# Inverting the triangular blocks of an RWKV-7 layer by 16x16 on VectorE, and applying the blocks beside them on TensorE

## The chip, the cores and the metric

The kernel runs on one core of a Trainium2 chip. The metric is the device time of one execution in microseconds (us). The engines are TensorE (PE; its weight loads are PEld), VectorE (DVE), ScalarE (ACT), GpSimd (POOL) and SyncE (SP), which issues the transfers.

## What is computed

One layer of a hybrid decoder: norms, dilated attention and RWKV-7 time mixing side by side, a gated merge, and a squared-ReLU MLP, for 1024 tokens of width 1024. The RWKV-7 part has 16 heads of 64 and a state that runs over all tokens. The change touches the RWKV-7 part alone:

```python
def wkv7_scan(r, w, k, v, a, b):
    """S_t = S_{t-1} diag(w_t) + (S_{t-1} a_t) b_t^T + v_t k_t^T ; y_t = S_t r_t."""
    ...
    def step(state, inp):
        r_t, w_t, k_t, v_t, a_t, b_t = inp
        sa = jnp.einsum('bhvk,bhk->bhv', state, a_t)
        state = (state * w_t[:, :, None, :] + sa[..., None] * b_t[:, :, None, :]
                 + v_t[..., None] * k_t[:, :, None, :])
        return state, jnp.einsum('bhvk,bhk->bhv', state, r_t)
    _, ys = lax.scan(step, s0, xs)
```

## The kernel before

The scan is not run step by step. The sequence is cut into 16 chunks of 64 tokens. Inside a chunk, what each token reads of the others is a strictly triangular 64x64 system, for each chunk and head; its solution gives the chunk as one matrix, and only a product for each chunk is then left to be done in order. The 16 heads are worked in 8 pairs (`m` = 0 to 7), two heads on the 128 partitions.

A pair goes through steps that `ORDER` names by letters: P projects r, k and v (dense products, L307); E and F make the decays and features; g (`pair_gram`, L749 to L757) makes the triangular systems `lm`; V the values (L722, L729); I (`pair_inverse`) inverts; L (`pair_local`) solves; C (`pair_chain`, L874, L877) runs over the chunks in order; N normalizes; G is a gate product of another part of the layer, dense products again. Tile, the layer in which the kernel is written, plans the order of all instructions on each engine when the program is built, with priorities that follow the order in which they are written, and each engine then runs its own list in that order. Dense products of P and G that are ready stand between the small products of the other steps. Nine gates (G7 to G15) stand behind the last pair in `ORDER`.

The triangular system of a chunk has two diagonal blocks of 32x32 (index `f`) and one block of 32x32 below. `pair_inverse` first turns `lm` by VectorE's transposes (L769) so that a partition holds one block of one chunk and head: 64 partitions, 32 x 32 elements in `lb`. Then a loop over `s` from 1 to 30 eliminates column by column: a product into a scratch (L775) and an addition (L777), each (31 - s) x s elements long. GpSimd writes the diagonal (L778), and two transposes (L781) bring the inverse back as `tt`. Meanwhile TensorE transposes `bk` (L785).

`pair_local` lays four chunks each as blocks of 32 on the diagonal of 128x128 operands `bd` (`place`, L805): `bd` 0 and 2 are the inverses of the two diagonal blocks, `bd` 1 the block below. It brings the right sides into `xx` by TensorE's transposes (L816, L820) and ScalarE's copies (L817, L822). Then come three rounds for each of two heads, each of four 128x128 products in float32 (L838; two records in the trace for each product): the inverse of the first block, the block below added to the second half (L840), the inverse of the second block. Results are copied to `x[0]` (L843) and to `eh` (L845). L853 to L858 make the chunk matrices from them.

Buffers that matter: pool `f4` hands out the tiles named `lt` in rotation over `NLT` = 3 buffers; in the order of the program these are `lb`, `tt`, the two `xx`, `y` and `sq` for each pair. Tiles named `ft` rotate over `NFT` = 6. `psS` has two PSUM buffers, which the small products share, `psD` has two for the dense ones. Weights are split into two parts: ScalarE casts (L64), GpSimd or VectorE subtracts (L65); `shifted` empties a projection by ScalarE (L542) and VectorE (L543).

Of the kernel before, what the change touches and what calls it, by code (L numbers as in the profile page):

```python
# [8 lines left out]
F32 = mybir.dt.float32  # L9
# [4 lines left out]
OP = mybir.AluOpType  # L14
# [19 lines left out]
NBD, NFT, NLT, NW, NGT, NRK = 5, 6, 3, 4, 2, 4  # L34
# [15 lines left out]
class Block:  # L50
# [22 lines left out]
    def pool(self, es, name, bufs, **kw):  # L73
        if kw.get("space") is not DRAM:
            kw["reuse_waits"] = "tile"
        return es.enter_context(self.tc.tile_pool(name=name, bufs=bufs, **kw))
# [469 lines left out]
    def rwkv(self, cst, wp, psD, oS, gS):  # L546
        nc, tc = self.nc, self.tc
        with ExitStack() as es:
            pool = lambda n, b, **kw: self.pool(es, n, b, **kw)
            rc, f4, b8, psC = pool("rc", 1), pool("f4", 4), pool("b8", 3), pool("psC", 1, space=PSUM)  # L550
            psS = pool("psS", 2, space=PSUM)
            self.omu = omu = rc.tile([128, 26], F32, name="omu")
            nc.vector.tensor_scalar(omu, self.c("shift_mu", 0, 26), -1.0, 1.0, op0=OP.mult, op1=OP.add)

            half = rc.tile([128, 4, 8], F32, name="half")
            for i, nm in enumerate(("decay_w0", "iclr_a0", "k_a")):
                nc.vector.tensor_scalar(half[:, i, :], self.c(nm, 0, 8), 0.5, None, op0=OP.mult)
            nc.vector.tensor_scalar(half[:, 3, :], half[:, 2, :], -1.0, 1.0, op0=OP.mult, op1=OP.add)
            smask = rc.tile([128, 8, 64], BF16, name="smask")
            nc.gpsimd.memset(smask, 1.0)  # L560
            nc.gpsimd.memset(smask[:, :, 0:1], 0.0)
            lnb = rc.tile([128, 1], F32, name="lnb")
            nc.vector.memset(lnb, 10.0 * math.log(2.0))

            dws = rc.tile([128, S], F32R, name="dws")
            das = rc.tile([128, S], F32R, name="das")
            dgs = rc.tile([128, S], F32, name="dgs")
            t = f4.tile([128, S], F32, name="rkv", bufs=NRK)
            p = self.project(wp, psD, C_LORA)
            self.shifted(p, t, 24)  # L570
            nc.scalar.activation(t[0:64], t[0:64], AF.Tanh)
            nc.scalar.copy(dws[0:64], t[0:64])
            nc.vector.tensor_tensor(dws[64:128], t[0:64], dws[0:64].bitcast(F32), OP.subtract)
            nc.scalar.copy(das[64:128], t[64:128])
            nc.vector.tensor_tensor(das[0:64], t[64:128], das[64:128].bitcast(F32), OP.subtract)
            p = self.project(wp, psD, C_LORA + 128)
            self.shifted(p, dgs, 25)
            nc.scalar.activation(dgs, dgs, AF.Tanh, scale=0.5)
            nc.vector.tensor_scalar(dgs, dgs, 0.5, 0.5, op0=OP.mult, op1=OP.add)

            bd = [rc.tile([128, 4, 128], F32, name=f"bd{i}") for i in range(NBD)]
            for b_ in bd:
                nc.gpsimd.memset(b_, 0.0)
            st = dict(rc=rc, f4=f4, b8=b8, bd=bd, dws=dws, das=das, dgs=dgs, smask=smask, half=half, lnb=lnb,
                      wp=wp, psD=psD, psS=psS, psC=psC, oS=oS, nbd=0)
            prs, step = {}, dict(
                P=lambda m: prs.__setitem__(m, self.pair_project(st, m)),
                E=lambda m: self.pair_lora(st, prs[m], m),
                F=lambda m: self.pair_features(st, prs[m], m),
                g=lambda m: self.pair_gram(st, prs[m], m),  # L590
                V=lambda m: self.pair_values(st, prs[m], m),
                I=lambda m: self.pair_inverse(st, prs[m], m),
                L=lambda m: self.pair_local(st, prs[m], m),
                C=lambda m: self.pair_chain(st, prs[m], m),
                N=lambda m: self.pair_norm(st, prs.pop(m), m),
                G=lambda j: self.gate(wp, psD, gS, j))
            for word in ORDER.split():
                if word[0] != "G" or int(word[1:]) >= NGA:
                    step[word[0]](int(word[1:]))
# [160 lines left out]
    def pair_inverse(self, st, pr, m):  # L760

        nc = self.nc
        f4, psS = st["f4"], st["psS"]
        bk, lm, fe = pr["bk"], pr["lm"], pr["fe"]

        lb = f4.tile([64, 32, 32], F32, name="lt", bufs=NLT)
        for f in range(2):
            fs = slice(32 * f, 32 * f + 32)
            nc.vector.transpose(lb[fs], lm[fs, f].rearrange("j u t -> j t u"))  # L769
        tt = f4.tile([64, 32, 32], F32, name="lt", bufs=NLT)  # L770
        pd = tt.rearrange("u t c -> u (t c)")
        for s in range(1, 31):
            n = 31 - s
            q = pd[:, 0:n * s].rearrange("u (t c) -> u t c", c=s)
            nc.vector.tensor_tensor(q, lb[:, s + 1:32, s:s + 1].to_broadcast([64, n, s]),  # L775
                                    lb[:, s:s + 1, 0:s].to_broadcast([64, n, s]), OP.mult)
            nc.vector.tensor_tensor(lb[:, s + 1:32, 0:s], lb[:, s + 1:32, 0:s], q, OP.add)  # L777
        nc.gpsimd.memset(lb.rearrange("u t c -> u (t c)")[:, 0:1024:33], 1.0)  # L778
        for f in range(2):
            fs = slice(32 * f, 32 * f + 32)  # L780
            nc.vector.transpose(tt[fs].rearrange("s u t -> s t u"), lb[fs].rearrange("u t s -> u t s"))  # L781
        for b in range(4):
            p = psS.tile([128, 4, 128], F32, name="s")
            for c in range(4):
                nc.tensor.transpose(p[:, c, :], bk[:, 4 * b + c].rearrange("p a t -> p (a t)"), self.ident)  # L785
            for h in range(2):
                nc.scalar.copy(fe[b // 2][:, h, 4 * (b % 2):4 * (b % 2) + 4, 64:128], p[:, :, 64 * h:64 * h + 64])
        pr["tt"] = tt

    def pair_local(self, st, pr, m):  # L790

        nc = self.nc
        f4, b8, psS = st["f4"], st["b8"], st["psS"]
        ident, ar, ar4, lm, fe, tt = self.ident, pr["ar"], pr["ar4"], pr["lm"], pr["fe"], pr["tt"]
        bds, ehs = [], []
        for h in range(2):
            bd = [st["bd"][(st["nbd"] + i) % NBD] for i in range(3)]
            st["nbd"] += 3
            bds.append(bd)

        def place(i, h):
            src = (tt[0:32], lm[0:32, 1], tt[32:64])[i]
            for q in range(4):
                qs = slice(32 * q, 32 * q + 32)
                (nc.scalar.copy if q % 2 or i == 1 else nc.vector.tensor_copy)(  # L805
                    bds[h][i][qs, :, qs], src[:, 16 * h + q:16 * h + 16:4, :])

        for h in range(2):
            place(1, h)
        xx = [f4.tile([128, 2, 4, 128], F32, name="lt", bufs=NLT) for h in range(2)]  # L810
        for f in range(2):
            for h in range(2):
                p = psS.tile([128, 4, 128], F32, name="s")
                for g in range(4):
                    u = slice(16 * h + 4 * g, 16 * h + 4 * g + 4)
                    nc.tensor.transpose(p[:, g, :], lm[:, f, u, :].rearrange("p u t -> p (u t)"), ident)  # L816
                nc.scalar.copy(xx[h][:, f, :, 0:64], p[:, :, 64:128])  # L817
            p = psS.tile([128, 4, 128], F32, name="s")
# [4 lines left out]
        for h in range(2):  # L823
            place(0, h)
        xs = [[x[:, 0], x[:, 1]] for x in xx]
        for h in range(2):
# [1 line left out]
            nc.gpsimd.memset(eh[64:128, :, 64:128], 0.0)  # L828
            nc.gpsimd.tensor_copy(eh[64:128, :, 0:64], ident[64:128, None, 64:128].to_broadcast([64, 16, 64]))
            ehs.append(eh)  # L830
        for i in range(3):
            for h in range(2):
                if i == 1:
                    place(2, h)
                x = xs[h]
                p = psS.tile([128, 4, 128], F32, name="s")
                for g in range(4):
                    nc.tensor.matmul(p[:, g, :], bds[h][i][:, g, :], x[i // 2][:, g, :], start=True, stop=True)  # L838
                if i == 1:
                    nc.vector.tensor_tensor(x[1], x[1], p, OP.add)  # L840
                else:
                    if i == 0:
                        nc.scalar.copy(x[0], p)  # L843
                    for q in range(4):
                        (nc.scalar.copy if i == 2 else nc.vector.tensor_copy)(  # L845
                            ehs[h][16 * i:16 * i + 32, q:16:4, :], p[32 * q:32 * q + 32])
        for b in range(4):
            for h in range(2):
                hp = slice(64 * h, 64 * h + 64)
                p = psS.tile([128, 4, 128], F32, name="s")  # L850
# [561 lines left out]
```

## Time and profile before

| | us |
|---|---|
| median of 3 runs | 2252.92 (2249.39 to 2259.89) |
| the profiled execution | 2252.45 |
| its span, first to last instruction | 2250.7 |
| TensorE busy in the span | 2083.3 (93%) |
| VectorE | 1559.3 (69%) |
| ScalarE | 1035.0 (46%) |
| GpSimd | 602.6 (27%) |

Busy times are of the profiled execution. An engine's busy share is a mean over stages that differ: the RWKV part lies between about 480 and 1340 us, and its stretches have to be read by themselves. The granted clock tells at which share of its full speed TensorE ran. Matmul records overlap, since a product begins before the one ahead of it has ended; distances from start to start tell the pace. Shares in lists of waits are idle time of an engine just before an instruction, put down to what released it last.

### The profile page before, as it was taken

To read this page: it belongs to the slowest core of one execution; us is meant where nothing else is said; L and a number is where in the kernel's file an instruction comes from. 1 tells how busy PE (TensorE), PEld (TensorE's weight loads), DVE (VectorE), ACT (ScalarE), POOL (GpSimd) and SP (SyncE) were. 2 spreads that over 40 slices of the span, in tenths; PEclk is the share of its full clock that TensorE was granted. 3 is DMA by queue.
4 is the path that set the end of the run, shared out by engine and by line. 5 is a ranking of instruction groups with operands and counts; after the bars stand their busy time and mean duration, and the time that the engine had idled before them with its cause. 6 is when DMAs were issued, how large, how long until landed. Compare 5 with 4: busy or idle time off the path is not lost. (4 is left out here: it accounts for less than half of the span.)

```text
span 2250.7 us, 28246 instructions
## 1 busy us (share of the span) xinstructions
PE 2083.3 (93%) x10002; PEld 1621.9 (72%) x10002; DVE 1559.3 (69%) x2857; ACT 1035.0 (46%) x2018; POOL 602.6 (27%) x455
## 2 busy tenths in 40 slices
PE   6899999988999989898989999999889999999997
PEld 2676766666777767676767778877667777788886
DVE  5845555458989787878777743436876553799988
ACT  4634533445454636454554442225744443533342
POOL 2504310321313131222122122201100000788850
PEclk9999999999999999999998999999999999999999
DMA  7513311110111110101011154432544333433232
GB/s 248 181 34 99 99 40 29 59 31 22 30 33 35 31 37 27 35 29 37 24 37 34 52 179 159 128 120 84 166 156 163 113 107 111 166 130 128 88 109 75
DMA packets 156315, 194.88 MB, mean 87 GB/s; under 512 B 10729, under 2 KB 110211, under 8 KB 154127
## 3 DMA queue, kind: packets, MB, share of 16 engines
q1 hardware_dynamic: 156175, 193.08, 25.8%
q8 instruction: 79, 1.29, 0.2%
q14 instruction: 61, 0.50, 0.1%
HBM read 152.14 MB, written 40.90 MB: 86 GB/s over the span
## 5 line engine op out<-in xcount | busy, mean ns | idle before, releaser
L307 PE MATMUL d<-hh,w_h 128*128 128x512 f32 x960 | 328.2, 414 | 8.0 <-ACT w_h L64 4.6
L307 PE MATMUL d<-hl,w_h 128*128 128x512 f32 x960 | 329.5, 413 | 2.9 <-DVE hl L280 2.9
L307 PE MATMUL d<-hh,w_l 128*128 128x512 f32 x960 | 324.2, 410 | 1.4 <-DVE w_l L65 1.3
L65 POOL TENSOR_TENSOR w_l<-w_t,w_h 128x256 fp32r<-128x256 f32 x160 | 128.3, 803 | 634.0 <-ACT w_h L64 288.7
L1108 PE MATMUL m<-op 128*128 128x512 f32 x1272 | 292.0, 391 | 6.3 <-DVE big L1344 2.4
L1108 PE MATMUL m<-big,op 128*128 128x512 f32 x1152 | 276.6, 401 | 8.0 <-ACT op L64 4.1
L1108 PEld LDWEIGHTS m<-op 128*128 128x128 f32 x1272 | 239.5, 189 | 58.5 <-POOL op L65 3.4
L1108 PEld LDWEIGHTS m<-big,op 128*128 128x128 f32 x1152 | 213.9, 189 | 70.8 <-DVE u L1219 5.3
L64 ACT CAST w_h<-w_t 128x256 fp32r<-128x256 f32 x272 | 108.4, 404 | 310.3 <-PE d L307 222.7
L307 PEld LDWEIGHTS d<-hh,w_h 128*128 128x128 f32 x960 | 180.4, 192 | 47.8 <-ACT w_h L64 5.8
L307 PEld LDWEIGHTS d<-hl,w_h 128*128 128x128 f32 x960 | 181.0, 192 | 44.9 <-issue 9.4
L307 PEld LDWEIGHTS d<-hh,w_l 128*128 128x128 f32 x960 | 180.1, 191 | 42.5 <-issue 7.9
L64 ACT CAST op<-t 128x512 fp32r<-128x512 f32 (+1 forms) x152 | 113.5, 775 | 174.5 <-PE m L1108 119.3
L153 POOL TENSOR_TENSOR macc<-macc,ada_t 128x512 f32<-128x512 f32 x56 | 87.2, 1559 | 179.5 <-ACT macc L151 160.7
L65 DVE TENSOR_TENSOR op<-t,op 128x512 fp32r<-128x512 f32 (+1 forms) x125 | 117.7, 962 | 20.5 <-ACT op L64 20.3
L1281 DVE TENSOR_TENSOR big<-big,m 128x1024 f32<-128x1024 f32 x88 | 104.7, 1210 | 11.9 <-PE m L1108 11.8
L1299 POOL TENSOR_TENSOR t<-big 128x1024 f32<-128x1024 f32 x7 | 23.1, 3303 | 325.8 <-DMA big<-in_w_ff_dram 325.4
L775 DVE TENSOR_TENSOR lt<-lt 64x30 f32<-64x30 f32 (+14 forms) x240 | 97.1, 404 | 8.2
L777 DVE TENSOR_TENSOR lt<-lt 64x30 f32<-64x30 f32 (+14 forms) x240 | 93.9, 391 | 7.7
L874 PEld LDWEIGHTS ch<-sv,fe 128*128 128x128 f32 x512 | 83.0, 190 | 20.2 <-DVE sv L877 8.9
L65 POOL TENSOR_TENSOR op<-t,op 128x1024 fp32r<-128x1024 f32 x27 | 88.4, 3275 | 7.1 <-ACT op L64 7.1
L65 DVE TENSOR_TENSOR w_l<-w_t,w_h 128x256 fp32r<-128x256 f32 x112 | 60.1, 545 | 40.3 <-ACT w_h L64 28.9
(381 smaller groups left out, 3888.4 us busy)
## 6 DMA issues: line engine op xcount, KB each, us to landing
w_t<-in_w_in_dram SPq DMA_DIRECT2D x240, 128.0 KB
ada_t<-in_ada_w_dram SPq DMA_DIRECT2D x64, 256.0 KB
fS<-ft SPq DMA_DIRECT2D x64, 256.0 KB
t<-in_w_ff_dram SPq DMA_DIRECT2D x16, 1024.0 KB
big<-fS SPq DMA_DIRECT2D x16, 1024.0 KB
big<-in_w_ff_dram SPq DMA_DIRECT2D x16, 1024.0 KB
x<-in_x_dram SPq DMA_DIRECT2D x16, 512.0 KB
ada_t<-in_ada_w_dram SPq DMA_DIRECT2D x16, 512.0 KB
```

Of the source, the lines that this page charges most:

```text
L64: nc.scalar.copy(hi, t)
L65: (eng or nc.vector).tensor_tensor(lo, t, hi.bitcast(F32), OP.subtract)
L153: nc.gpsimd.tensor_tensor(acc, acc, t, OP.add)
L307: nc.tensor.matmul(p[:, 512 * half + cs.start:512 * half + cs.stop], a, b[half][k][:, cs], start=k == ks[0] and i == 0, stop=k == ks[-1] a ...
L775: nc.vector.tensor_tensor(q, lb[:, s + 1:32, s:s + 1].to_broadcast([64, n, s]), lb[:, s:s + 1, 0:s].to_broadcast([64, n, s]), OP.mult)
L777: nc.vector.tensor_tensor(lb[:, s + 1:32, 0:s], lb[:, s + 1:32, 0:s], q, OP.add)
L874: nc.tensor.matmul(ps[h][:, c8, :], fe[b][:, h, c8, :], sv[h][b][:, c8, :], start=True, stop=True)
L1108: self.nc.tensor.matmul(p, s, m, start=start and k == 0 and i == 0, stop=k == len(a) - 1 and i == 2, skip_group_check=not start)
L1281: nc.vector.tensor_tensor(acc[nm][h], acc[nm][h], ps2[h], OP.add)
L1299: vb.tensor_tensor(t3, wr[:, k2, h2], wr[:, k1, h2], OP.subtract)
```

## The change

The inverse is made for blocks of 16x16 in place of 32x32. Each diagonal block of 32 is seen as two diagonal blocks of 16 and one block of 16 below them. The loop on VectorE runs over `s` from 1 to 14 and treats both blocks of 16 in one operation (a fourth dimension `b` of 2), 2 x (15 - s) x s elements long. GpSimd clears the block below in `lb` before the transposes back, so that `tt` holds the inverses of the blocks of 16 alone. The blocks of 16 below are placed into four new operands `nb` (by head and `f`) from `lm`, and the solve applies inverse, block below, inverse again, for each of the two halves, with the 32x32 block between: seven rounds (`n` = 0 to 6) with the operands 0, 3, 0, 1, 2, 4, 2. The results of rounds 0 and 4 go to a scratch `xt` from the `ft` rotation by ScalarE; those of rounds 1, 3 and 5 are added on VectorE. `lb` becomes a tile of its own, outside of the `lt` rotation. Of the four copies of round 2 into `eh`, one for each head moves from VectorE to ScalarE.

```diff
@@ rwkv
-            for b_ in bd:
+            nb = [[rc.tile([128, 4, 128], F32, name=f"nb{h}{f}") for f in range(2)] for h in range(2)]
+            for b_ in bd + nb[0] + nb[1]:
                 nc.gpsimd.memset(b_, 0.0)
@@ pair_inverse
-        lb = f4.tile([64, 32, 32], F32, name="lt", bufs=NLT)
+        lb_ = f4.tile([64, 1056], F32, name="lb", bufs=1)
+        lb = lb_[:, 0:1024].rearrange("u (t c) -> u t c", c=32)
...
-        for s in range(1, 31):
-            n = 31 - s
-            q = pd[:, 0:n * s].rearrange("u (t c) -> u t c", c=s)
-            nc.vector.tensor_tensor(q, lb[:, s + 1:32, s:s + 1].to_broadcast([64, n, s]),
-                                    lb[:, s:s + 1, 0:s].to_broadcast([64, n, s]), OP.mult)
-            nc.vector.tensor_tensor(lb[:, s + 1:32, 0:s], lb[:, s + 1:32, 0:s], q, OP.add)
-        nc.gpsimd.memset(lb.rearrange("u t c -> u (t c)")[:, 0:1024:33], 1.0)
+        l4 = lb_.rearrange("u (b x) -> u b x", b=2)[:, :, 0:512].rearrange("u b (t c) -> u b t c", c=32)
+        for s in range(1, 15):
+            n = 15 - s
+            q = pd[:, 0:2 * n * s].rearrange("u (b t c) -> u b t c", b=2, c=s)
+            nc.vector.tensor_tensor(q, l4[:, :, s + 1:16, s:s + 1].to_broadcast([64, 2, n, s]),
+                                    l4[:, :, s:s + 1, 0:s].to_broadcast([64, 2, n, s]), OP.mult)
+            nc.vector.tensor_tensor(l4[:, :, s + 1:16, 0:s], l4[:, :, s + 1:16, 0:s], q, OP.add)
+        nc.gpsimd.memset(lb[:, 16:32, 0:16], 0.0)
+        nc.gpsimd.memset(lb_[:, 0:1024:33], 1.0)
@@ pair_local
         def place(i, h):
+            if i > 2:
+                f = i - 3
+                for q in range(4):
+                    (nc.scalar.copy if q % 2 else nc.vector.tensor_copy)(
+                        st["nb"][h][f][32 * q:32 * q + 16, :, 32 * q + 16:32 * q + 32],
+                        lm[32 * f:32 * f + 16, f, 16 * h + q:16 * h + 16:4, 16:32])
+                return
...
         for h in range(2):
-            place(1, h)
+            for i in (1, 3, 4):
+                place(i, h)
...
-        for i in range(3):
+        xt = [st["f4"].tile([128, 8, 65], F32, name="ft", bufs=NFT).rearrange("p a b -> p (a b)")[:, 0:512]
+              .rearrange("p (g t) -> p g t", t=128) for h in range(2)]
+        for n, i in enumerate((0, 3, 0, 1, 2, 4, 2)):
             for h in range(2):
-                if i == 1:
+                if n == 2:
                     place(2, h)
                 x = xs[h]
                 p = psS.tile([128, 4, 128], F32, name="s")
+                bd = bds[h][i] if i < 3 else st["nb"][h][i - 3]
+                y = (x[0], xt[h], x[0], x[0], x[1], xt[h], x[1])[n]
                 for g in range(4):
-                    nc.tensor.matmul(p[:, g, :], bds[h][i][:, g, :], x[i // 2][:, g, :], start=True, stop=True)
-                if i == 1:
-                    nc.vector.tensor_tensor(x[1], x[1], p, OP.add)
+                    nc.tensor.matmul(p[:, g, :], bd[:, g, :], y[:, g, :], start=True, stop=True)
+                if n in (0, 4):
+                    nc.scalar.copy(xt[h], p)
+                elif n in (1, 3, 5):
+                    nc.vector.tensor_tensor(x[n > 1], x[n > 1], p, OP.add)
                 else:
-                    if i == 0:
+                    if n == 2:
                         nc.scalar.copy(x[0], p)
                     for q in range(4):
-                        (nc.scalar.copy if i == 2 else nc.vector.tensor_copy)(
+                        (nc.scalar.copy if n > 2 or q == 3 else nc.vector.tensor_copy)(
                             ehs[h][16 * i:16 * i + 32, q:16:4, :], p[32 * q:32 * q + 32])
```

## Rows read from the trace of the kernel before

**Rows 1.** The page's first part: busy us, share, instructions of each engine.
```profile
PE 2083.3 (93%) x10002; PEld 1621.9 (72%) x10002; DVE 1559.3 (69%) x2857; ACT 1035.0 (46%) x2018; POOL 602.6 (27%) x455
```

**Rows 2.** Busy times by stretch: the RWKV part; then granted clock, DMA share, GB/s.
```profile
480.00:1340.00 860.00, 777.24 (x4191) 620.32 (x4191) 685.53 (x1514) 435.58 (x900) 198.86 (x236) 0.94 0.13 39
```

**Rows 3.** Waits of TensorE, 480 to 1340 us: total us, times, longest.
```profile
PE s L816 <- ACT lt L817: 36.8, 8, 6.1
PE s L749 <- DVE fe L757: 8.3, 4, 2.5
...
PE s L853 <- ACT b L845: 4.8, 7, 1.2
...
PE s L816 <- DVE rkv L730: 0.2, 1, 0.2
```

**Rows 4.** Groups by line: count, busy us, mean ns, idle before and releaser.
```profile
L775 DVE TENSOR_TENSOR lt<-lt 64x30 f32<-64x30 f32 (+14 forms) x240 | 97.1, 404 | 8.2
L777 DVE TENSOR_TENSOR lt<-lt 64x30 f32<-64x30 f32 (+14 forms) x240 | 93.9, 391 | 7.7
...
L838 PE MATMUL s<-lt,bd 128*128 128x128 f32 x384 | 56.0, 301 | 0.2
...
L845 DVE COPY b<-s 32x512 f32<-32x512 f32 x64 | 43.8, 685 | 2.8 <-ACT lt L843 1.9
...
L805 DVE COPY bd<-lt 32x128 f32<-32x128 f32 x64 | 15.9, 248 | 18.8 <-PE s L838 17.6
...
L843 ACT COPY lt<-s 128x512 f32<-128x512 f32 x16 | 9.2, 583 | 5.5 <-PE s L838 5.1
```

**Rows 5.** Timeline of all engines at the end of one inverse: start, duration, instruction.
```profile
840.99 0.61 PE L307 MATMUL d<-hh,w_l 128*128 128x512 f32 x2
...
842.51 3.83 DVE L781 STREAM_TRANSPOSE lt<-lt 32x1024 f32<-32x1024 f32 x2
844.44 1.25 ACT L805 COPY bd<-lt 32x128 f32<-32x128 f32 x4 [5.97 <-DVE lt L781]
845.71 0.41 ACT L64 CAST w_h<-w_t 128x256 fp32r<-128x256 f32 x1
...
846.86 0.47 PE L816 MATMUL s<-ident,b 128*128 128x128 f32 x1 [5.25 <-ACT lt L817]
```

**Rows 6.** Timeline of TensorE in two solves.
```profile
746.66 3.07 PE L838 MATMUL s<-lt,bd 128*128 128x128 f32 x24
749.48 0.71 PE L307 MATMUL d<-hh,w_l 128*128 128x512 f32 x2
...
855.59 1.05 PE L838 MATMUL s<-lt,bd 128*128 128x128 f32 x8
856.40 0.71 PE L307 MATMUL d<-hh,w_h 128*128 128x512 f32 x2
856.94 0.62 PE L307 MATMUL d<-hl,w_h 128*128 128x512 f32 x2
857.40 0.61 PE L307 MATMUL d<-hh,w_l 128*128 128x512 f32 x2
```

**Rows 7.** Timeline of VectorE and GpSimd in one inverse.
```profile
912.50 0.20 DVE L775 TENSOR_TENSOR lt<-lt 64x30 f32<-64x30 f32 x1
...
914.96 2.48 POOL L908 TENSOR_TENSOR lt<-lt,rkv 128x1024 f32<-128x1024 f32 x1 [5.48 <-ACT lt L904]
915.25 2.36 DVE L775 TENSOR_TENSOR lt<-lt 64x150 f32<-64x150 f32 x1
...
928.13 0.40 DVE L777 TENSOR_TENSOR lt<-lt 64x240 f32<-64x240 f32 x1
```

**Rows 8.** TensorE behind a wait for the inverse (two of eight), and at 861 us.
```profile
538.60:546.60 8.00, 6.24 (x32) 0.78 0.00 0
...
1271.00:1279.00 8.00, 7.97 (x39) 0.69 0.06 16
...
861.00:868.00 7.00, 5.64 (x32) 3.96 (x31) 2.49 (x4) 6.58 (x12) 0.00 (x0) 1.00 0.14 54
```

More of the change, by code (lines that the diff above doesn't have):

```diff
@@ L581, in rwkv @@
             bd = [rc.tile([128, 4, 128], F32, name=f"bd{i}") for i in range(NBD)]
-            for b_ in bd:
+            nb = [[rc.tile([128, 4, 128], F32, name=f"nb{h}{f}") for f in range(2)] for h in range(2)]
+            for b_ in bd + nb[0] + nb[1]:
                 nc.gpsimd.memset(b_, 0.0)
-            st = dict(rc=rc, f4=f4, b8=b8, bd=bd, dws=dws, das=das, dgs=dgs, smask=smask, half=half, lnb=lnb,
+            st = dict(rc=rc, f4=f4, b8=b8, bd=bd, nb=nb, dws=dws, das=das, dgs=dgs, smask=smask, half=half, lnb=lnb,
                       wp=wp, psD=psD, psS=psS, psC=psC, oS=oS, nbd=0)
```

## The prediction

> **What bounds the kernel now.** I read the page's engine totals first, then one stretch that holds the part which the change touches, then who TensorE waited for in it. TensorE is busy 93% of the span, VectorE 69% [rows 1]. The RWKV part, in which all eight inverses and solves lie, is the stretch from 480 to 1340 us: TensorE 777 of 860 us, VectorE 686, ScalarE 436, at a mean granted clock of 0.94 [rows 2]. So TensorE sets the pace there, with 83 us of idle time and about 860 x 0.06 = 52 us lost to the lower of its two clock levels (1.2 in place of 2.4 GHz). Whatever is saved on another engine counts only as far as it takes some of this 135 us away; whatever is added to TensorE counts in full, because work that waits for nothing (the gate products) is left over and still fills TensorE after the last pair.
>
> Of the 83 us, 36.8 us are eight waits of one kind, one in each pair: the transposes of L816 for the copy of L817. Another 24.7 us are eight rows released by VectorE, the first 8.3, the last 0.2 [rows 3]. The timeline of one pair shows how the first kind comes about [rows 5]: TensorE ends its dense work at 841.6 and stands still until 846.9. VectorE is in the last steps of the inverse and its two transposes back (842.5 to 846.3). ScalarE stands in order behind them with the copies into `bd`, and behind these stand the next cast of a weight (845.7), without which no dense product starts, and the copy into `xx` (L817), whose buffer is the one that the inverse still reads (`lt` rotates over three). The granted clock in the 8 us behind such a wait is 0.63 to 0.79, eight such windows, first 0.78 and last 0.69 [rows 8]; summed, (1 - clock) x 8 us is 17 us. So the inverse costs TensorE 37 us idle and 17 us of slow clock, 54 us in all. That is the most that shortening the inverse can return directly.
>
> **The change part by part.**
>
> *The inverse.* Before: 240 + 240 operations, 97.1 + 93.9 us [rows 4], 60 operations and 23.9 us a pair. After: 14 steps of two operations, 28 to 112 elements wide (both blocks of 16 together, 2 x s x (15 - s)), in sum 2240 elements. The operation at 30 elements takes 0.20 us, at 240 elements 0.40 [rows 7]: 0.17 us and 0.95 ns per element. 28 x 0.17 + 2240 x 0.00095 = 6.9 us a pair. The bounds: 28 x 0.20 = 5.6 us, and 28 x 0.40 = 11.3 us at the mean of the lines now, which holds waits on GpSimd (one operation of 150 elements took 2.36 us while GpSimd's L908 ran [rows 7]). VectorE gives up 17 us a pair, 136 us in eight. The chain from the gram to the solve gets some 17 to 18 us shorter. The transposes (L769, L781) stay. GpSimd gets one more memset a pair; it waits for VectorE's transposes, and GpSimd's weight subtractions stand behind it, as they do behind L778 now, only for less long.
>
> *`lb` leaves the rotation.* `lt` then holds `tt`, two `xx`, `y`, `sq`; the second `xx` takes the buffer of the previous pair's `sq` instead of the inverse's own. The transposes L816 and L820 need not wait for the inverse. What is late next is `bd` from `tt`, that is, the first product of the solve.
>
> *The solve.* Three rounds become seven: 4 more rounds x 2 heads x 4 products, 8 groups of 4 products (8 records) a pair, 64 groups in all. A run of 24 records starts at 746.66 and the next product at 749.48, 0.94 us a group; the nearest low row is 0.81 (855.59 to 856.40) [rows 6]; the nearest high one 56.0 us / 48 groups = 1.17, with slow clock in it [rows 4]. I take 0.94: +60 us on TensorE (52 to 75), all on the engine that sets the pace. A switch from these to the dense products costs 0.08 us: two dense products take 0.54 us from start to start right behind a group and 0.46 us in the run [rows 6]. With one or two more switches a round, 8 x 4 x 1.5 x 0.08 = +4 us (0 to 10).
>
> *Around the solve.* VectorE gets 32 more additions of 512 columns (0.685 each by L845, as wide; 22 us) and 64 small copies (0.248 for the nearest, L805; 16 us), and loses 16 copies of L845 (0.685 each, 11 us) [rows 4]. Its net is -136 + 27 = -109 us, from 80% to 67% of the stretch. ScalarE gets 32 copies of 0.583 (19 us) [rows 4], 64 small ones of 1.25 / 4 = 0.31 us [rows 5] (20 us), and those 16 (9 us): +48 us, 51% to 56%. Neither becomes the bound. The small copies need only the gram and lie beside the inverse. The new copies and additions lie inside the solve: each has the other head's group beside it. One round is 0.94 us of products for a head, and a copy of 0.58 or an addition of 0.69 behind them; the other head's 0.94 us covers it, if the copying engine comes at once. Dense products are the further cover. Some of the dense work now spent beside the inverse is free for this. The added zeroing before the first pair (four tiles on GpSimd) is hidden: nothing is in the solve by then.
>
> *What comes back.* Of the 36.8 us wait I take 31 away (20 to 37): the order on each engine is fixed when the program is built, and the wait is what the inverse really took beyond what that order had allowed for; with 28 operations in place of 60 about a sixth to a half of that excess may remain, now ahead of L838. Of the 17 us of clock, 14 come back (6 to 17), since the clock does not fall behind short stops: the stretch that holds a stop of 1.2 us before L853 is granted 1.00 [rows 3, 8]. Of the 24.7 us of VectorE-released waits and the clock lost elsewhere (52 - 17 = 35 us), 13 us together (0 to 37): VectorE is free 109 us more, but these waits lie in the gram and the value stage, where its work doesn't change. New waits of ScalarE's and VectorE's evacuations in the longer solve: +3 us (0 to 20; the nearest row, L853 behind L845, 4.8 us in 7 waits, at most 1.2 us each [rows 3]).
>
> The sum: 60 + 4 - 31 - 14 - 13 + 3 = +9 us. The profiled execution took 2252.45 us (span 2250.7), within 0.5 us of the median 2252.92, so the forecast is 2262 us.
>
> **The rivals.**
>
> *Rival 1, faster: the freed VectorE takes the other waits along.* For it: 24.7 us are released by VectorE in stages where it is nearly full, and each long one is followed by slow clock. Against: their producers aren't touched. The whole 37 + 17 us, 25 us of waits and a third of the other 35 us of clock (12) go: 60 + 4 - 37 - 17 - 25 - 12 = -27, 2225 us.
>
> *Rival 2, slower: TensorE stands between the rounds.* The place is the four added rounds, each of which ends in a copy that a busy ScalarE or VectorE must make before the next product. It decides from the point where the evacuation comes later than the other head's 0.94 us and no dense product is left in the order there. Price: one wait of 1.2 us a pair [rows 3], 10 us, and a granted clock as in the worst window of the eight now, 0.63 [rows 8], 8 x 0.37 = 3 us a pair, 24 us in place of today's 17. 60 + 4 - 31 + 7 + 10 = +50, 2302 us. Against: within the solves of [rows 6] TensorE doesn't stand still. The Trainium skill (TensorE: Matmul & The Clock Gate, A second HAM failure mode: psum-queue depth-cycling) has the rule that short idle times between groups of products cycling through PSUM make the clock swing between its levels; by that rule this rival is the case, while the trace has shown a fall only behind longer stops.
>
> *Rival 3: the change doesn't do what it says.* The order is built anew and TensorE stands before L838 as long as it now does before L816, with the weight's cast behind `bd` on ScalarE as before: 60 + 4 + 3 = +67, 2319 us.
>
> **How the numbers follow.** About 0.5% (11 us) is what a measurement of this kernel can tell from no change. The forecast's own case, 2240 to 2282, holds 0.50: 0.31 within 0.5%, 0.17 slower, 0.02 faster, since +9 lies close to the upper edge. Rival 1 holds 0.25, rival 2 0.18, rival 3 0.07. Faster 0.02 + 0.25 = 0.27; within 0.31; slower 0.17 + 0.18 + 0.07 = 0.42. The range reaches to rivals 1 and 2, 2222 to 2302, and leaves out the third and the tails. The bounds of all terms together would be 52 + 0 - 37 - 17 - 37 + 0 = -39 and 75 + 10 - 20 - 6 - 0 + 20 = +79; they would have to fall together, so the range doesn't go that far.
>
> **What would show it.** In the changed kernel: L775 and its partner at 224 operations together for eight pairs and some 55 us; TensorE's wait before L816 gone, at most some 6 us in sum before L838; the solve's product records 896 in place of 384, and some 60 us more TensorE busy time between 480 us and the end of the part; VectorE near 67%. The forecast is wrong on the low side if the idle time of the stretch falls well below 40 us with a mean clock over 0.97, and on the high side if waits for the solve's copies sum to more than 10 us or the clock in the solves is below 0.8. It would also be wrong if TensorE's added work were hidden, that is, if fewer than some 50 us of added busy time appeared.

## The result, and the profile after

| | before | after |
|---|---|---|
| median, us | 2256.4 (2249.39 to 2262.46) | 2354.44 (2350.01 to 2359.98) |
| ratio, 95% interval | 1 | 1.0437 [1.0396, 1.0478] |
| profiled execution / its span, us | 2252.45 / 2250.7 | 2350.01 / 2348.3 |
| mean granted clock of the execution | 0.97 | 0.96 |

The runs of both kernels together were timed anew, so that the median of before stands a little above the one given ahead. The changed kernel is 98 us slower. The prediction, 2262 us with a range of 2222 to 2302, was wrong: too low, and the time lies outside of the range.

The first part of the page after; [rows 1] is its match.

```profile
PE 2171.1 (92%) x10514; PEld 1695.2 (72%) x10514; DVE 1467.1 (62%) x2681; ACT 1081.8 (46%) x2130; POOL 614.4 (26%) x467
```

The RWKV part, from 480 us to the last dense product, ends at another time in each kernel, so it is read here from 480 us to its own end. The columns are those of [rows 2]: start and end, length, busy time of TensorE, its weight loads, VectorE, ScalarE and GpSimd, granted clock, DMA share, GB/s. Before:

```profile
480.00:1364.20 884.20, 801.44 (x4298) 640.35 (x4298) 693.71 (x1521) 446.33 (x916) 204.72 (x242) 0.95 0.14 45
```

After:

```profile
480.00:1457.90 977.90, 891.15 (x4808) 714.13 (x4807) 606.02 (x1345) 492.12 (x1028) 214.28 (x250) 0.93 0.13 41
```

The part is 93.7 us longer, of the 97.6 us by which the whole span is. TensorE's busy time grew by 89.7 us and its idle time by 4.0 (82.8 to 86.8). VectorE gave up 88 us. So the loss is busy time of TensorE, and the lines tell which. After (count, busy us, mean ns, idle before and its releasers); L854 answers to L838, L892 to L874, L750 to L749, L828 to L816, L778 and L780 to L775 and L777:

```profile
L892 PE MATMUL ch<-sv,fe 128*128 128x64 f32 x512 | 91.8, 279 | 7.1 <-DVE sv L895 7.0
L854 PE MATMUL s<-lt,bd 128*128 128x128 f32 x640 | 88.3, 292 | 15.0 <-ACT bd L816 12.0 <-DVE bd L816 1.8 <-DVE lt L858 0.6
L750 PE MATMUL s<-ar,b 64*128 64x128 f32 x512 | 79.9, 354 | 27.5 <-DVE fe L758 22.5 <-DVE ar L710 4.2 <-DVE rsg_t L141 0.8
L854 PE MATMUL s<-ft,nb 128*128 128x128 f32 x256 | 35.3, 296 | 0.0
L778 DVE TENSOR_TENSOR lt<-lb 64x28 f32<-64x28 f32 (+6 forms) x112 | 31.0, 277 | 3.3
L780 DVE TENSOR_TENSOR lb<-lb,lt 64x28 f32<-64x28 f32 (+6 forms) x112 | 29.6, 265 | 3.5
```

The same groups of TensorE before, for the chain and the gram:

```profile
L874 PE MATMUL ch<-sv,fe 128*128 128x64 f32 x512 | 82.8, 260 | 2.1 <-DVE sv L877 1.6
L749 PE MATMUL s<-ar,b 64*128 64x128 f32 x512 | 68.7, 313 | 13.8 <-DVE fe L757 8.3 <-DVE ar L709 2.5 <-DVE rsg_t L140 2.3
```

The solve takes 88.3 + 35.3 = 123.6 us in place of 56.0 [rows 4]: +67.6 for 896 records in place of 384. The other 22 us (89.7 - 67.6) are products that the change doesn't touch, as many as before, which take longer: 9.0 in the chain, 11.2 in the gram, the rest in small pieces. Of the wait before L816 of [rows 3], 36.8 us, 1.9 are left:

```profile
PE s L828 <- ACT lt L829: 1.9, 1, 1.9
```

The transposes of L832 wait another 2.7 us for the same copy, 13.8 us stand before L854 now, where 0.2 stood before L838 [rows 4], and the gram's wait grew from 8.3 to 22.5.

### The profile page after: what moved, and what is told of

Its sections match the earlier page's. It is cut to its first block, busy times and chain, and to the rows that moved or that the text cites. A ratio compares the mean times of both kernels' runs of the same rounds, so it can differ in the third digit from the quotient of the medians.

```text
span 2348.3 us, 29231 instructions
## 1 busy us (share of the span) xinstructions
PE 2171.1 (92%) x10514; PEld 1695.2 (72%) x10514; DVE 1467.1 (62%) x2681; ACT 1081.8 (46%) x2130; POOL 614.4 (26%) x467
## 3 DMA queue, kind: packets, MB, share of 16 engines
q1 hardware_dynamic: 156175, 193.08, 24.7%
## 5 line engine op out<-in xcount | busy, mean ns | idle before, releaser
L307 PE MATMUL d<-hl,w_h 128*128 128x512 f32 x960 | 324.8, 413 | 0.0
L65 POOL TENSOR_TENSOR w_l<-w_t,w_h 128x256 fp32r<-128x256 f32 x160 | 135.5, 848 | 720.6 <-ACT w_h L64 463.2
L895 DVE TENSOR_SCALAR sv<-ch,dd 64x64 f32<-64x64 f32 x240 | 64.3, 290 | 89.1 <-PE ch L892 86.5
L892 PEld LDWEIGHTS ch<-sv,fe 128*128 128x128 f32 x512 | 91.9, 207 | 36.3 <-DVE sv L895 22.7
L750 PE MATMUL s<-ar,b 64*128 64x128 f32 x512 | 79.9, 354 | 27.5 <-DVE fe L758 22.5
L854 PE MATMUL s<-lt,bd 128*128 128x128 f32 x640 | 88.3, 292 | 15.0 <-ACT bd L816 12.0
L750 PEld LDWEIGHTS s<-ar,b 64*128 64x128 f32 x512 | 68.7, 246 | 44.0 <-issue 33.9
```

The costliest lines, as they stand in the source:

```text
L65: (eng or nc.vector).tensor_tensor(lo, t, hi.bitcast(F32), OP.subtract)
L307: nc.tensor.matmul(p[:, 512 * half + cs.start:512 * half + cs.stop], a, b[half][k][:, cs], start=k == ks[0] and i == 0, stop=k == ks[-1] a ...
L750: nc.tensor.matmul(ps[h][:, c, :].rearrange("p (a t) -> p a t", t=32), bk[hp, cc].rearrange("p a t -> p (a t)"), ar4[hp, :, cc, :], start= ...
L854: nc.tensor.matmul(p[:, g, :], bd[:, g, :], y[:, g, :], start=True, stop=True)
L892: nc.tensor.matmul(ps[h][:, c8, :], fe[b][:, h, c8, :], sv[h][b][:, c8, :], start=True, stop=True)
L895: nc.vector.tensor_scalar(sv[h][(c + 1) // 8][64:128, (c + 1) % 8, :], ps[h][64:128, c8, :], dd[64:128, h, c:c + 1], None, op0=OP.mult)
```

## What the slow products are

The mean clock fell from 0.95 to 0.93. Summed over windows of 1 us, (1 - clock) x length is 48 us of the part before and 70 after, and these 22 us more are the 22 us of slower products. By place, the chains went from 2 to 21 us, the grams from 15 to 36, and everything else, with the stretches behind the old wait for the inverse, from 31 to 13. How it comes about is seen in a pair's chain. Before, chain products (L874) stand between the products of the chunk matrices (L853), the decays' (L652) and the dense ones; timeline of TensorE, start, duration, instruction:

```profile
866.89 1.16 PE L853 MATMUL s<-fe,b 128*128 128x128 f32 x8
867.89 0.33 PE L874 MATMUL ch<-sv,fe 128*128 128x64 f32 x2
868.03 0.48 PE L652 MATMUL d<-das,lorah 128*128 128x512 f32 x1
```

```profile
868.00:884.00 16.00, 15.52 (x98) 12.48 (x96) 14.20 (x36) 11.78 (x18) 0.95 (x1) 1.00 0.03 9
```

After, the chunk matrices (L871) come first, then 14 us of nothing but dense products, then the chain (L892) with little between its steps, each of which waits for VectorE's L895, the operation that takes the step before out of PSUM (its evacuation):

```profile
1012.96 1.05 PE L871 MATMUL s<-fe,b 128*128 128x128 f32 x8
1013.77 0.71 PE L307 MATMUL d<-hl,w_h 128*128 128x512 f32 x2
...
1030.39 0.66 PE L892 MATMUL ch<-sv,fe 128*128 128x64 f32 x4 [0.16 <-DVE sv L895]
1031.21 0.66 PE L892 MATMUL ch<-sv,fe 128*128 128x64 f32 x4 [0.16 <-DVE sv L895]
1032.03 0.43 PE L892 MATMUL ch<-sv,fe 128*128 128x64 f32 x2 [0.16 <-DVE sv L895]
```

The stretches of that pair after: the solve from its fourth microsecond on, the dense block, the chain, and inside the chain four microseconds by themselves; last the gram of the next pair, whose first product waited 3.4 us.

```profile
984.00:1001.00 17.00, 16.93 (x123) 15.55 (x122) 9.84 (x15) 9.05 (x18) 1.46 (x2) 0.98 0.06 16
1014.00:1028.00 14.00, 14.00 (x64) 11.57 (x63) 3.04 (x6) 4.07 (x8) 3.68 (x5) 1.00 0.17 49
1028.00:1044.00 16.00, 15.52 (x58) 11.19 (x57) 9.20 (x24) 8.84 (x13) 0.79 (x2) 0.68 0.14 48
1036.00:1040.00 4.00, 4.00 (x11) 2.75 (x11) 2.53 (x6) 2.18 (x4) 0.00 (x0) 0.50 0.02 4
1062.00:1078.00 16.00, 12.37 (x50) 10.09 (x51) 9.46 (x28) 1.52 (x2) 4.88 (x4) 0.65 0.06 18
```

The chain has a TensorE that is busy 15.52 of 16 us, as busy as before, and a clock of 0.68 in place of 1.00. From 1036 to 1040 TensorE doesn't stop at all and runs at 0.50, which is the lower of its two levels, 1.2 GHz: behind a chain of small products with stops of 0.16 us. This is busy time that the profile counts as work. The fall does not come in every pair: of the six chains after that stand behind such a block, four were granted 0.79 from first to last product and took 24.7 us each, and two, in the same order, 1.00 and took 21.1. Before, seven of the eight chains were granted 1.00 and one 0.92.

The order in which TensorE's instructions stand in one of the middle pairs, counted from both kernels in products (D dense, T transposes, M chunk matrices, C chain, E decays; all runs of the middle are given, the gram before and the rest of the chain behind are left out):

```
before  ... D75 T8 D1 T4 solve4 D1 solve4 D13 solve4 D7 solve12 D6 M4 D4 M4 D2 M4 D1 M4 C2 E1 M4 C2 E1 C2 E1 M8 C2 ...
after   ... D15 solve24 D13 solve4 D3 solve4 D2 solve24 D6 M4 D4 M4 D2 M4 D1 M4 D2 M4 D1 M4 D2 M4 D1 M4 D64 C2 E2 C7 E1 C1 E1 ...
```

Before, 75 dense products lay beside the long inverse and few were left for later. With the short inverse only 15 do; the dense work that P and G hold ahead of C in `ORDER` is then put as one block of 64 between M and C, and the chain stands almost alone: it has lost its cover, the dense products that filled its waits. Whether this order, and not something else of the change, costs the time is what the experiments ask.

## Experiments

The two theories told apart first: the *work theory* (the prediction's: TensorE pays the products, the short inverse gives time back) and the *order theory* (the short inverse gives little or nothing back, since the planned order around it gets worse). Differences are to the kernel before in runs on the same chip, about 2255 us. The numbers of a kernel's part are of its own window from 480 us to its last dense product.

**The added rounds alone: `rounds_only`.** The changed kernel with the old inverse of 32x32, `lb` in the `lt` rotation; the blocks beside stay zero, so that all seven rounds run and the result is the same.

```diff
-        for s in range(1, 15):
+        for s in range(1, 31):
...
-            for i in (1, 3, 4):
-                place(i, h)
+            place(1, h)
```

> The changed kernel with the inverse of before: blocks of 32x32 on VectorE, in the lt rotation. The four operands nb stay zero, so the four added rounds run in full (256 products more, their copies and additions) and add nothing to the result. Order theory (the short inverse no longer covers the dense products, which then go ahead of the chain over the chunks): the order around the inverse stays as before, so only the products are paid for, about 60 us: 2305 to 2325 us. Work theory (the added products cost far more than 0.94 us a group and are the whole loss): the whole 98 us appears here, 2345 us or more. In both TensorE's wait ahead of the solve stays.

Measured: 2328.94 us, 1.0323 [1.0302, 1.0344], +73.

```profile
480.00:1433.60 953.60, 866.86 (x4808) 700.91 (x4807) 700.11 (x1536) 473.68 (x964) 208.54 (x242) 0.95 0.13 42
```

TensorE's busy time grows by 65.4 us and its idle time by 4.0; the clock stays at 0.95. The products cost what the prediction counted for them, some 6 us more, and nothing hides them. It also leaves some 25 us to the changed kernel, in which VectorE has far less to do: with seven rounds the short inverse and its buffer make the kernel slower, not faster.

**Half of the added rounds: `five_rounds`.** `rounds_only` without the two rounds that were added to the second half.

```diff
-        for n, i in enumerate((0, 3, 0, 1, 2, 4, 2)):
+        for n, i in ((0, 0), (1, 3), (2, 0), (3, 1), (6, 2)):
```

> rounds_only with added rounds for the first half alone: five rounds in place of seven, the inverse of before, nb zero, the result unchanged; 128 products more than before in place of 256. If the added products are paid for one by one on TensorE, half of rounds_only's 73 us: 2285 to 2297 us. If a first added round already breaks the order and the rest is cheap, 2305 us or more; if the rounds are hidden up to some number, 2270 us or less.

Measured: 2290.64 us, 1.0156 [1.0132, 1.018], +35: half of 73. Half of the added products cost half of the time; no step shows between three, five and seven rounds.

**The short inverse alone: `inverse_only`.** The kernel before with the new inverse, `lb` its own tile as in the change, and three rounds. The blocks of 16 beside the diagonal are left out of the computation.

```diff
-        for s in range(1, 31):
...
+        l4 = lb_.rearrange("u (b x) -> u b x", b=2)[:, :, 0:512].rearrange("u b (t c) -> u b t c", c=32)
+        for s in range(1, 15):
...
```

> The kernel before with the inverse of the changed one alone: blocks of 16x16, lb as a tile of its own, three rounds, no nb. It leaves out the blocks of 16 beside the inverted ones. VectorE has 136 us less to do and TensorE nothing more. Work theory: the wait for the inverse and the slow clock behind it go, 2200 to 2225 us. Order theory: the 60 or so dense products that stood beside the inverse now stand between the chunk matrices and the chain, the chain loses their cover, and the gain is lost or turned around: 2280 to 2300 us (the changed kernel's 2354 less 60).

Measured: 2266.72 us, 1.0045 [1.003, 1.006], +11. Neither theory's number, but on the order theory's side: VectorE is busy 117 us less in the part (693.71 to 576.80), and the kernel is slower.

```profile
480.00:1377.40 897.40, 826.62 (x4284) 653.35 (x4284) 576.80 (x1263) 446.40 (x911) 210.78 (x250) 0.92 0.14 45
```

```profile
L877 PE MATMUL ch<-sv,fe 128*128 128x64 f32 x512 | 93.4, 283 | 6.3 <-DVE sv L880 6.3
L749 PE MATMUL s<-ar,b 64*128 64x128 f32 x512 | 79.2, 354 | 27.7 <-DVE fe L757 22.6 <-DVE ar L709 4.2 <-DVE rsg_t L141 0.8
```

Idle time falls by 12.0 us (82.8 to 70.8), as it should, but TensorE is busy 25.2 us longer with no product added, at a clock of 0.92: 10.6 us in the chain (82.8 to 93.4), 10.5 in the gram (68.7 to 79.2). These are the slow products of the changed kernel, without the new rounds. Its planned order has the same shape: 61 dense products in one block ahead of the chain. The same kernel with `lb` in the rotation was not run, so what the buffer alone costs (next) is in these numbers.

**The buffer alone: `lb_own`.** The kernel before, with `lb` a tile of its own.

```diff
-        lb = f4.tile([64, 32, 32], F32, name="lt", bufs=NLT)
+        lb = f4.tile([64, 32, 32], F32, name="lb", bufs=1)
```

> The kernel before with one edit: lb as a tile of its own, outside of the lt rotation. Order theory: the inverse is as long as before and covers the dense products as before, so within 0.7% of before: 2240 to 2272 us. Rival (it is the rotation that orders the work anew, since the copies into xx no longer wait for the inverse): a good part of the loss is here, 2285 us or more. Theory of the prediction: TensorE's wait of 37 us moves from the transposes to the first product of the solve, 2250 us.

Measured: 2278.76 us, 1.0114 [1.0079, 1.015], +23, between the two. What TensorE waits for:

```profile
PE s L838 <- ACT bd L805: 19.1, 4, 5.5
PE s L838 <- DVE bd L805: 15.7, 3, 5.3
```

The transposes L816 no longer wait, and the first product of the solve waits 34.8 us in place of 36.8. Freeing the buffer moves the wait and hardly shortens it. The part's clock is 0.93 in place of 0.95; the gram's products are busy 76.0 us in place of 68.7, those of the solve 60.4 in place of 56.0.

**`lb` back in the rotation: `after_lb_in_rotation`.** The same buffer undone in the changed kernel.

```diff
-        lb_ = f4.tile([64, 1056], F32, name="lb", bufs=1)
+        lb_ = f4.tile([64, 1056], F32, name="lt", bufs=NLT)
```

> The changed kernel with lb back in the lt rotation. lb_own alone made the kernel before 23 us slower. If that loss is part of the changed kernel's 98 us, 2325 to 2338 us. If it came only because the long inverse then stood ahead of the solve (35 us of waits before the first product of the solve in lb_own, 12 in the changed kernel), it doesn't come back: 2345 to 2360 us. Its planned order still has 52 dense products ahead of the chain in place of 64, so the chain stays uncovered.

Measured: 2342.34 us, 1.0399 [1.0365, 1.0432], 12 us below the changed kernel, whose interval it overlaps. The buffer is a small part of the loss at most.

**The chain ahead of the dense work: `chain_first`.** The changed kernel with each C from C1 to C6 written ahead of the next pair's P and of G.

```diff
-... I1 V1 L1 P2 G1 C1 E2 ...
+... I1 V1 L1 C1 P2 G1 E2 ...
```

> The changed kernel with one edit: in ORDER each C(m) from C1 on stands ahead of P(m+1) and G(m) in place of behind them. The work is the same. Order theory: the chain starts beside the chunk matrices again and has dense products as its cover; 20 to 40 us come back, 2315 to 2335 us, less if E and F of the next pair lose their cover in turn. Work theory: the time doesn't move, 2345 to 2365 us.

Measured: 2323.3 us, 1.0294 [1.0279, 1.0309], 31 us below the changed kernel.

```profile
480.00:1434.30 954.30, 861.00 (x4824) 687.85 (x4823) 615.64 (x1347) 491.42 (x1032) 211.62 (x250) 0.96 0.13 42
```

```profile
L892 PE MATMUL ch<-sv,fe 128*128 128x64 f32 x512 | 80.2, 256 | 0.1
L750 PE MATMUL s<-ar,b 64*128 64x128 f32 x512 | 63.1, 327 | 31.6 <-DVE fe L758 29.1 <-DVE ar L710 2.5
```

```profile
996.75 1.13 PE L871 MATMUL s<-fe,b 128*128 128x128 f32 x8
997.72 0.34 PE L892 MATMUL ch<-sv,fe 128*128 128x64 f32 x2
997.86 0.48 PE L307 MATMUL d<-hl,w_h 128*128 128x512 f32 x1
998.18 1.05 PE L871 MATMUL s<-fe,b 128*128 128x128 f32 x8
```

The chain stands between other products again; it loses its wait (7.1 to 0.1 us) and its slow clock (all eight chains are granted 1.00; 91.8 to 80.2 us), and the clock of the part rises to 0.96. The gram gets quicker too (79.9 to 63.1), with waits that are longer than before the edit, so its slowness isn't made by its own wait alone; but part of it stays, since (1 - clock) x length over the grams is 24 us here, 36 in the changed kernel and 15 before. TensorE is idle longer than in the changed kernel (93.3 against 86.8 us) and still done 24 us sooner.

**The same on the short inverse alone and on the kernel before: `inverse_chain_first`, `before_chain_first`.** The same edit of `ORDER`; the first of them leaves the blocks of 16 beside out, as `inverse_only` does.

> The short inverse alone (three rounds, the blocks of 16 beside left out, as in inverse_only) with each C(m) ahead of P(m+1) and G(m) in ORDER. Order theory: inverse_only lost its gain to the uncovered chain, mostly as slow clock; with the cover back it is 30 us faster than inverse_only, 2225 to 2245 us, and so clearly faster than before. Rival (the wait for the inverse was never worth more than it gave; the clock falls elsewhere anyway): 2255 to 2270 us.

> The kernel before with each C(m) ahead of P(m+1) and G(m) in ORDER, nothing else. Control for chain_first. With the long inverse the dense products of P and G still have the inverse as their place, so the order theory expects little: 2240 to 2275 us. If the order of the words is worth 30 us by itself, 2215 to 2235 us.

Measured: `inverse_chain_first` 2231.32 us, 0.9906 [0.9873, 0.9938], 35 us below `inverse_only`. `before_chain_first` 2263.47 us, 1.0038 [1.0014, 1.0062], +8.

```profile
480.00:1345.10 865.10, 786.62 (x4309) 624.76 (x4308) 587.85 (x1266) 446.26 (x918) 207.61 (x250) 0.96 0.15 46
```

The edit of `ORDER` is worth 31 to 35 us where the inverse is short and costs 8 where it is long. So this part of the loss is made by the two together: the short inverse lets go of the dense work, and `ORDER` then puts it ahead of the chain. With the order mended, the short inverse is worth 25 us to the kernel before.

**Both undone: `chain_first_lb_in_rotation`.**

> The changed kernel with both: each C(m) ahead of P(m+1) and G(m), and lb back in the lt rotation. If the two are separate, 31 + 12 us come back: 2305 to 2318 us. The floor by the order theory is inverse_chain_first plus the price of the rounds: 2231 + 60 to 73 = 2291 to 2304 us; below that the price of the rounds would be wrong. It can't reach before.

Measured: 2315.19 us, 1.026 [1.0234, 1.0286], the lowest of the changed kernel's forms, though `chain_first` lies within its error. It stays 61 us above the kernel before. `rounds_only`'s 73.4 less `inverse_chain_first`'s 24.6 is +49, so some 12 us are left that neither part has by itself; the rounds cost more than any order here gave back.

**The gate alone behind the chain: `gate_behind_chain`.** The changed kernel with only G moved.

```diff
-... P2 G1 C1 E2 ...
+... P2 C1 G1 E2 ...
```

> The changed kernel with G(m) alone moved behind C(m); P(m+1) stays ahead. The planned order has 28 dense products between the chunk matrices and the chain in place of 64, and dense products beside all of the chain. If the cover beside the chain is what counts, about as chain_first, 2315 to 2335 us; if the chain's nearness to the chunk matrices counts, about half of its gain, 2335 to 2345 us.

Measured: 2344.58 us, 1.0379 [1.0339, 1.042], 10 us below, with an interval that overlaps the changed kernel's. Its trace is of the longest of its executions, 2355.51 us. The chain's products are quick (82.9 us, mean 251 ns), but TensorE waits elsewhere; its waits for these three were 2.0, 0.0 and 4.2 us in the changed kernel:

```profile
PE ch L929 <- ACT lt L922: 12.7, 12, 1.4
PE ch L918 <- POOL ft L697: 11.4, 6, 2.0
PE s L730 <- DVE rkv L731: 8.8, 8, 1.7
```

A dense product that covers the chain can't also cover the normalization and the values. That the gain was lost because it was moved from these to the chain is a reading of these waits; no run tests it.

**What the wait for the inverse was made of: `subtract_on_vector`, `bonus_on_vector`.** The prediction puts the long wait before L816 down to an inverse that takes longer than the order had allowed for, and part of the time of its operations to GpSimd's work beside them [rows 7]. The first kernel takes the weight subtractions of r, k and v from GpSimd to VectorE, the second the addition of L908, which the long operation of [rows 7] ran beside. Both start from the kernel before.

```diff
-            p = self.project(st["wp"], st["psD"], C_RWKV + 1024 * i + 128 * m, self.nc.gpsimd)
+            p = self.project(st["wp"], st["psD"], C_RWKV + 1024 * i + 128 * m)
```

```diff
-        nc.gpsimd.tensor_tensor(o, o, pr["bv"], OP.add)
+        nc.vector.tensor_tensor(o, o, pr["bv"], OP.add)
```

> The kernel before with one edit: the subtraction of the split weights of P goes to VectorE in place of GpSimd. It asks whether TensorE's 36.8 us of waits for the inverse are what the inverse took beyond its place in the planned order because VectorE waited on GpSimd. If so, the wait before L816 falls below 20 us although VectorE has some 50 us more to do, 2225 to 2250 us. If the wait has another cause, it stays at 30 us or more, 2250 to 2285 us.

> The kernel before with one edit: the addition of the bonus in pair_norm (L908, 2.4 us on GpSimd, beside which one operation of the inverse took 2.36 us in place of 0.31) goes to VectorE. If the wait for the inverse is VectorE's waiting on GpSimd, some 2 us a pair go: the wait before L816 falls to 18 to 24 us and the time to 2225 to 2248 us. If not, the wait stays at 30 us or more, 2250 to 2270 us.

Measured: `subtract_on_vector` 2274.49 us, 1.0087 [1.0058, 1.0117]; `bonus_on_vector` 2250.01 us, 0.9966 [0.9946, 0.9986]. The waits, first and second:

```profile
PE s L816 <- ACT lt L817: 32.3, 8, 4.6
```

```profile
PE s L816 <- ACT lt L817: 39.4, 8, 6.2
```

```profile
L775 DVE TENSOR_TENSOR lt<-lt 64x30 f32<-64x30 f32 (+14 forms) x240 | 89.3, 372 | 7.8
```

In the second the products of the inverse take 7.8 us less (97.1 to 89.3), and TensorE waits 39.4 us in place of 36.8. Neither of these two pieces of GpSimd's work by itself makes the wait; both moved together were not run. `bonus_on_vector` is the one kernel with the whole result that came out below the kernel before, by 0.3%, less than the 0.5% that the prediction takes for telling.

## Why the prediction was wrong, step by step

**The products: right.** 60 + 4 + 3 = 67 us against +73 in `rounds_only` and half of it for half of the rounds. The products alone, 60 (52 to 75) in the sum, are 67.6 us of busy time in the changed kernel. TensorE is the engine that sets the pace, its added work was not hidden, and the waits in the solve are 0.6 us in sum for the additions (L854 behind L858). The clock in the solves was no lower than before: 0.91 over five of the eight, each behind a wait before its first product, 1.00 over three, where before it lay between 0.86 and 0.98.

**VectorE's saving: right for the loop, and worth nothing in this order.** The loop takes 31.0 + 29.6 = 60.6 us in 224 operations, where 55 were forecast. Its net saving in the part is 87.7 us, where 109 were forecast; that it went to 62% and not 67% comes from the longer part.

**The wait before L816: right in kind, 21 us in place of 31.** 1.9 us of it are left, and 13.8 us came back before L854, where at most 6 had been named (36.8 - 1.9 - 13.8 = 21.1; 18 if the 2.7 us before L832 are counted too). `lb_own` shows that the buffer by itself hardly shortens the wait, which then stands before L838 (34.8 us); it takes the shorter loop.

**The clock and the other waits: the step that failed.** The sum had -14 for the clock behind the long wait and -13 for other waits and clock, and bounded both so that at worst 6 and 0 us came back; a loss was not among the bounds. The clock behind the long wait did come back: outside of chains and grams 18 us less is lost to the clock. What failed is that the clock fell anew elsewhere, by 18 us in the chains and 22 in the grams. Measured with the inverse alone: -12.0 us of idle time and +25.2 us of the same products run slower; for the whole of "what comes back" -58 was forecast, and `inverse_only` came out at +11. Two sentences failed. "Some of the dense work now spent beside the inverse is free for this" was read as a gift to the solve. The work was indeed let go, but the planner put it where `ORDER` ranks it, in a block ahead of the chain, and took the chain's cover away. And "the clock does not fall behind short stops" was drawn from one stop of 1.2 us, before L853 in the stretch at 861 us [rows 8]. The same trace speaks against it: in another pair the same line waits 1.21 us, until 1074.81, and from 1075 to 1084 the clock is 0.50.

```profile
1074.00:1086.00 12.00, 11.19 (x42) 8.41 (x43) 6.88 (x13) 7.36 (x13) 0.00 (x0) 0.57 0.00 1
```

So one stop that left the clock alone was no ground for a rule; rival 2's remark that the trace showed a fall only behind longer stops falls with it. In the changed kernel's chains a row of stops of 0.16 us was enough in four pairs. `chain_first` and `inverse_chain_first`, which change the order alone, take back 31 and 35 us.

**What is late next** was answered for the solve alone. The gram of the next pair waits 22.5 us in place of 8.3 for features made on VectorE; it does so in every kernel looked at here with the short inverse (22.6 in `inverse_only`, 29.1 in `chain_first`). The clock behind one such wait is 0.65, and the grams hold 22 of the 40 us by which chains and grams lost more to the clock. The order of C mends this half only in part. That VectorE, done sooner with the inverse, has other operations planned ahead of the features is a possible cause; it was not tried.

**The rivals.** Rival 1 fell: TensorE's waits released by VectorE, 24.7 us before, are 44.9 in the changed kernel, the gram's 22.5 first. Rival 2 had the mechanism and not the place. Between the rounds TensorE doesn't stand. But the clock did go to its lower level with short stops at products that wait for an evacuation, in the chain. The Trainium skill (TensorE: Matmul & The Clock Gate, A second HAM failure mode: psum-queue depth-cycling) has this rule, that frequent short idling between groups of products makes the clock swing. The trace agrees with it in four of the six chains without cover (0.68 in the stretch shown, stops of 0.16 us) and not in the other two (1.00); the solve, which has no such stops between its rounds, doesn't test it. Rival 3 had it that the order is built anew to no good; that much was so, though TensorE doesn't stand before L838 as it said (15.0 us against 36.8).

**The size.** The part's +93.7 us is 67.6 of products, 22 of products run slower and 4.0 of idle time. Even the upper bound of all terms together, +79, was too low for the 98 us, since no term of the sum allowed for a loss by the clock.

**What stays open.** `rounds_only` and `inverse_only` sum to +84 of 98 us; the other 14 are little more than what the intervals of the three leave open. In the profiles the rest is idle time: the inverse takes 12.0 us of it from the kernel before and none from `rounds_only` (86.7 to 86.8). By place, the changed kernel waits longer than `inverse_only` by 6.7 us before the transposes of the solve (L828, 8.4 against 1.7), 2.3 before the solve, 1.9 in the values, and less elsewhere. Why these come back with seven rounds is not settled, nor why two of the six chains without cover kept their clock, nor why the gram waits longer. Nor is it settled what the wait for the inverse before is made of, now that GpSimd's share has fallen.

## What to carry to other kernels

When a step on an engine that doesn't set the pace gets shorter, ask which work of the pacing engine was its cover, where the order will put that work now, and what loses its own cover for it. Read idle time and granted clock together: a chain of small products that each wait for an evacuation can show a TensorE that is busy 97% of the time at two thirds of its clock. And before work is moved to the pacing engine, try the step that saves alone: here it gave nothing until the order around it was mended.

## What the runs showed of the hardware

The clock can fall to its lower level in a stretch without any long stop. In the chain shown, three steps, each behind a stop of 0.16 us, came before it, and in the middle of the slow stretch TensorE was busy 4.00 of 4.00 us at 0.50. Four of six such chains went this way (0.79 over the whole chain); two kept 1.00. With dense products between the steps, all eight chains of `chain_first` and seven of eight in the kernel before were granted 1.00. The same stop of 1.21 us before L853 was followed by 1.00 in one pair of the kernel before and by 0.50 for 9 us in another. The mean of the short inverse's 28 operations was 271 ns (60.6 us / 224), where 246 (6.9 us / 28) had been worked out from single ones.
